# Residual stream of a hybrid layer with tokens on partitions; activations as the stationary operand in both output passes and the output projection; token chunks 272/384/384

## The chip, the cores and the metric

One core of a Trainium2 chip runs the whole layer. The metric is the device time of one launch in microseconds (us), the median of several runs; less is better. The core's engines work side by side and wait for one another by semaphores: TensorE (PE) multiplies matrices and writes to PSUM; VectorE (DVE), ScalarE (ACT) and GpSimd (POOL) work elementwise; SyncE (SP) issues most transfers, one after another, to the DMA engines. In a matmul, PE holds one operand of up to 128 x 128 (the stationary one, loaded by PEld) and streams the other (the moving one) column by column, up to 512 columns, into a PSUM tile.

## The reference

One layer for 1024 tokens of width 1024, with 16 learned tokens ahead of them (1040 rows in all), in float32:

```python
h = h + 0.5 * swiglu(rms_norm(h, ffn1_norm), ffn1_w_in, ffn1_w_out)
u = rms_norm(h, mix_norm) @ w_in
o = concat([hgrn2(...), stick_breaking(...)])     # two groups of heads, 512 columns each
h = h + o @ w_out
h = h + 0.5 * swiglu(rms_norm(h, ffn2_norm), ffn2_w_in, ffn2_w_out)
return h[:, 16 tokens on]
```

`swiglu` is `(silu(g) * u) @ w_out` with `g, u` the halves of `h @ w_in`; the FFN's inner width is 2816. The two mixers' insides are the same before and after.

## The kernel before

Every operand of a large product is split into a high and a low part ("wh, wl" for weights, "xh, xl", "th, tl" for activations: a cast on ACT, a subtraction on DVE), and each product is three matmuls (high x high, high x low, low x high). So each weight tile goes from its raw buffer (an SP transfer) through ACT (L277, L516, L148) and DVE (L279, L518, L150) to PE.

The residual stream is kept with the model's width on partitions: `hT` holds eight tiles of 128 features by all tokens. Tokens are cut into three chunks by `THIRDS` (352, 344 and 344 with the 16 learned ones in the first). The first FFN runs one chunk plainly, and the other two as a pair with seven products in place of eight: the operands are combined blocks (B11, B21, B22, T1 to T4; weights A11, A12, A22, S1 to S4), named after the step. Its stages in order:

- Input products, `fast_in`: for each weight tile the plain chunk (bank `qd`) and the pair (banks `qa`, `qb`, `qc`), 12 matmuls each. Meanwhile `turn_x` (L711) turns x by PE transposes (L721) into `xD` in DRAM.
- Output pass, `fast_out`: first `plain_round` (L554, 22 rows of weights with 24 matmuls each), then the seven products, each over 11 pairs of weight rows `q` (L588). The weights are stationary, the activations move; four PSUM tiles hold 4 x 128 features by 344 tokens, and at a step's end four DVE operations add them to `hT` (L598). `load_h` fetches `hT` from `xD` in eight transfers of 520 KB. Row sums for the norm (`norm_steps`) come from squares on ACT (L210), sums on DVE (L211), a PE product with a column of ones (`nps`, L176) and a PE product that spreads the result over partitions (`spread`, L199); the scaled result is split in two (L1449, L1454). `project_early` then begins the mixers' projections.
- Mixers, with a hand-set weave of PE work. `mix_out` (L1228) multiplies `o` by `w_out`: the first half (four heads, `oT`) is woven into the mixers' work, the second half (`oH`) follows, for each 128 columns `m` and for two token halves of 512. Its result goes to `hT` and `h2D` (DRAM). Weights of the second half come through the pool "wo2" with two raw buffers (`raw`, L141).
- Second FFN, over two token halves of 512 by the seven products alone: `blocks_a` and `blocks_b` make the combined blocks out of normed `hT`, `fast_in` and `fast_out` as above with 512 columns, and `store_out` (L732) turns the result by PE transposes (L739) into rows and stores it, after the steps S3 and A22.

PE's order is the order in which the code issues its work (`manual_schedule`); the other engines get theirs from a scheduler, and pools reuse memory, so that a transfer can wait for the last reader of what lay in its place. SP's queue is served in order: a transfer that waits holds up those behind it.

Of the kernel before, what the change touches and what calls it, by code (L numbers as in the profile page):

```python
# [28 lines left out]
THIRDS = [(0, 352), (352, 344), (696, 344)]  # L29
# [10 lines left out]
class Block:  # L40
# [19 lines left out]
    def setup(self):  # L60
# [19 lines left out]
        self.g2 = self.column(a["ffn2_norm"][0], KT, "g2")  # L80
# [144 lines left out]
    def blocks_a(self, hT, gain, c, n, r, ops):  # L225


        for half, o in enumerate(("B11", "B21")):
            for j in range(4):
                self.halve(ops[o], self.normed(hT, gain, 4 * half + j, c, n, r), j)  # L230
                yield

    def blocks_b(self, hT, gain, cs, n, r, ops, pool):

        nc = self.nc
        sub = nc.vector.tensor_sub
        b11, b21 = ([hT[:, k + j, cs[0] : cs[0] + n] for j in range(4)] for k in (0, 4))
        b12, b22, t2 = [], [], []  # L240
        for j in range(4):
            b12.append(self.normed(hT, gain, j, cs[1], n, r))
            b22.append(self.normed(hT, gain, 4 + j, cs[1], n, r))
            sub(b11[j], b12[j], b11[j])
            t2.append(pool.tile([P, n], F32, tag="nsq", name="t2", bufs=4))
            sub(t2[j], b22[j], b11[j])
            self.halve(ops["T2"], t2[j], j)
            if j < 3:
                yield
        for j in range(4):  # L250
            sub(b21[j], b21[j], t2[j])
        yield
        for j in range(4):
            sub(b12[j], b22[j], b12[j])
            self.halve(ops["T3"], b12[j], j)
        yield
        for o, b in (("T1", b11), ("T4", b21), ("B22", b22)):
            for j in range(4):
                self.halve(ops[o], b[j], j)
            yield  # L260
# [228 lines left out]
    def fast_out(self, hT, cs, n, w_out, actD, load_h, ready, between=lambda a, q: None,  # L489
# [6 lines left out]
        nq = D_FF // 256  # L496
        sk = op.tile([P, nq, 512], F32, name="sk")
# [46 lines left out]
        def plain_round():  # L544
            c0, n0 = plain
# [14 lines left out]
            for m in range(KT):  # L560
                h = hT[:, m, c0 : c0 + n0]
                nc.vector.scalar_tensor_tensor(h, ps[m], 0.5, h, ALU.mult, ALU.add)
# [12 lines left out]
        for bank, a, b, start, (i, j) in steps:  # L575
            if start:
                banks[bank] = [
                    pout.tile([P, n], F32, tag=f"{bank}{m}", name="o") for m in range(4)
                ]
            for q in range(nq):  # L580
                wh, wl = halved(left(a, q), "w", 512)
                xh, xl = halved(right((q, b), n), "t", n)
                order = [(m, e) for m in range(4) for e in range(3)]
                if a == "A12" and q == 0:
                    order.sort(key=lambda me: me[1])
                for m, e in order:
                    y, z = ((wh, xh), (wl, xh), (wh, xl))[e]
                    nc.tensor.matmul(  # L588
                        banks[bank][m], y[:, m * P : (m + 1) * P], z,
# [6 lines left out]
            for m in range(4):  # L596
                h = hT[:, 4 * i + m, cs[j] : cs[j] + n]
                self.evicted = nc.vector.scalar_tensor_tensor(  # L598
                    h, banks[bank][m], 0.5, h, ALU.mult, ALU.add
                )  # L600
            ready(a)
# [109 lines left out]
    def turn_x(self, pool, xD):  # L711

        nc = self.nc
        for r0 in range(0, T, P):
            m = min(P, T - r0)
# [15 lines left out]

    def store_out(self, hT, pool, pps, c0, n, tag):  # L732
        nc = self.nc
        for i, r0 in enumerate(range(c0, c0 + n, P)):
            for q in range(2):
                row = pool.tile([P, 512], F32, tag="orow", name="orow", bufs=4)
                ps = pps.tile([P, 4, P], F32, tag=f"{tag}{(2 * i + q) % 4}", name="o")
                for k in range(4):
                    nc.tensor.transpose(ps[:, k, :], hT[:, 4 * q + k, r0 : r0 + P], self.ident)  # L739
                dst = row.rearrange("p (k c) -> p k c", k=4)  # L740
                if q == 0:
# [593 lines left out]
    def run(self):  # L1335
# [20 lines left out]
        with ExitStack() as c0:  # L1356
            with ExitStack() as c1:
# [54 lines left out]
                with tc.manual_schedule(engines={nc.tensor.engine}), ExitStack() as c2:  # L1412
# [97 lines left out]
                    for _ in range(5):  # L1510
                        next(last)
# [205 lines left out]
```

## Time and profile before

| | |
|---|---|
| median of 3 runs | 2102.15 us (2101.22 to 2105.67) |
| span of the profiled execution, first to last instruction | 2101.1 us |
| lowest run, against that span | 0.1 us more |
| mean granted TensorE clock | 0.994 |
| 0 to 60 us, start: PE busy | 44.59 us |
| 60 to 500, first FFN's input products: PE busy | 436.21 us |
| 745 to 1380, projections and mixers: PE busy | 608.17 us |
| 1380 to 1430, second half of the output projection: PE busy, DVE busy | 46.77, 36.82 us |
| 1475 to 1875, second FFN's input products after their start: PE busy | 395.39 us |
| 1875 to 2066, second FFN's output pass: PE busy, DVE busy | 187.77, 136.55 us |

A line of the profile names an engine, a source line, the operation and its tiles as out<-in. In the chain of work, a row is "start, duration, what": the chain is followed back from the last instruction to what released it, so a row of DVE or DMA there is a time in which PE waited. In rows by stretches of time, each engine's busy time stands with its count of instructions; then the granted clock, the share of the DMA engines and GB/s. "idle <-" or "[... <-]" names what ended the wait before an instruction.

### The profile page before, as it was taken

To read this page: it belongs to the slowest core of one execution; us is meant where nothing else is said; L and a number is where in the kernel's file an instruction comes from. 1 tells how busy PE (TensorE), PEld (TensorE's weight loads), DVE (VectorE), ACT (ScalarE), POOL (GpSimd) and SP (SyncE) were. 2 spreads that over 40 slices of the span, in tenths; PEclk is the share of its full clock that TensorE was granted. 3 is DMA by queue.
4 is the path that set the end of the run, shared out by engine and by line. 5 is a ranking of instruction groups with operands and counts; after the bars stand their busy time and mean duration, and the time that the engine had idled before them with its cause. 6 is when DMAs were issued, how large, how long until landed. Compare 5 with 4: busy or idle time off the path is not lost.

```text
span 2101.1 us, 32170 instructions
## 1 busy us (share of the span) xinstructions
PE 2028.4 (97%) x11520; PEld 1830.6 (87%) x11520; DVE 1392.3 (66%) x2140; ACT 901.4 (43%) x1860; POOL 647.1 (31%) x710
## 2 busy tenths in 40 slices
PE   7999999999999999999999998998999999999998
PEld 6999999999999999988897887886788888878887
DVE  6875544555489942258878776659776676677674
ACT  8543333333465634456666514235233233234443
POOL 2475545452000002243334200012554464430000
PEclk9999999999999999999999999999999999999999
DMA  7643333325867635435454162234533332358364
GB/s 198 190 146 121 110 111 104 98 80 197 254 207 223 220 116 166 156 108 138 119 142 131 51 242 87 81 118 135 162 103 100 111 105 91 107 193 267 111 200 136
DMA packets 272566, 301.12 MB, mean 143 GB/s; under 512 B 24694, under 2 KB 199158, under 8 KB 272406
## 3 DMA queue, kind: packets, MB, share of 16 engines
q1 hardware_dynamic: 254710, 248.62, 39.1%
q0 software_dynamic: 16656, 50.44, 6.5%
q8 instruction: 91, 1.49, 0.3%
q14 instruction: 69, 0.57, 0.1%
q10 hardware_dynamic: 1040, 0.00, 0.0%
HBM read 216.42 MB, written 82.57 MB: 142 GB/s over the span
## 4 chain that ended last, share of the span: by engine, by line
PE 83%; DVE 7%; ACT 2%; issue 1%; DMA 0%; POOL 0%; SPq 0%; DVEq 0%; ACTq 0%; POOLq 0%
PE o L588 16%; PE qb L320 13%; PE qc L320 9%; PE qa L320 8%; PE qd L320 6%; PE proj L163 5%; PE proj L164 5%; PE proj L165 5%; PE o L554 4%; PE flip L1070 2%; PE lvl L839 2%; PE wo L164 1%; PE wo L163 1%; PE wo L165 1%; DVE keep L1216 1%
## 5 line engine op out<-in xcount | busy, mean ns | idle before, releaser
L320 PE MATMUL qb<-T,wh 128*128 128x344 f32 (+1 forms) x1056 | 311.6, 358 | 9.7 <-DVE u L362 5.8
L279 DVE TENSOR_TENSOR wl<-s,wh 128x512 fp32r<-128x512 f32 x176 | 202.5, 1151 | 112.6 <-ACT wh L277 109.9
L588 PE MATMUL o<-tl,wh 128*128 128x344 f32 (+1 forms) x616 | 219.1, 357 | 5.1 <-DVE tl L518 5.1
L320 PEld LDWEIGHTS qb<-T,wh 128*128 128x128 f32 x1056 | 193.0, 189 | 35.3 <-ACT wh L277 7.5
L588 PE MATMUL o<-th,wl 128*128 128x344 f32 (+1 forms) x616 | 218.8, 357 | 2.5 <-DVE wl L518 2.5
L588 PE MATMUL o<-th,wh 128*128 128x344 f32 (+1 forms) x616 | 218.6, 357 | 0.0
L320 PE MATMUL qa<-B,wh 128*128 128x344 f32 (+1 forms) x704 | 209.3, 361 | 0.0
L277 ACT CAST wh<-s 128x512 fp32r<-128x512 f32 x176 | 109.4, 622 | 224.5 <-PE qb L320 154.6
L163 PE MATMUL proj<-xh,wh 128*128 128x344 f32 (+2 forms) x576 | 204.9, 356 | 0.0
L164 PE MATMUL proj<-xh,wl 128*128 128x344 f32 (+2 forms) x576 | 199.5, 346 | 1.1 <-DVE wl L150 1.1
L165 PE MATMUL proj<-xl,wh 128*128 128x344 f32 (+2 forms) x576 | 198.7, 345 | 0.0
L279 DVE TENSOR_TENSOR wl<-raw,wh 128x512 fp32r<-128x512 f32 x172 | 153.4, 896 | 68.1 <-ACT wh L277 61.9
L277 ACT CAST wh<-raw 128x512 fp32r<-128x512 f32 x172 | 105.8, 620 | 194.0 <-PE qc L320 96.0
L320 PE MATMUL qb<-T,wl 128*128 128x344 f32 (+1 forms) x528 | 188.3, 357 | 0.0
L320 PE MATMUL qd<-X,wh 128*128 128x352 f32 x704 | 180.5, 324 | 1.3 <-DVE X L665 1.3
L516 ACT CAST th<-act 128x512 fp32r<-128x512 f32 (+2 forms) x176 | 95.2, 542 | 182.3 <-PE o L588 126.6
L292 POOL TENSOR_TENSOR s<-raw 128x512 f32<-128x512 f32 x88 | 125.0, 1421 | 94.4 <-DVE wl L279 70.1
L518 DVE TENSOR_TENSOR tl<-act,th 128x512 fp32r<-128x512 f32 (+2 forms) x176 | 105.7, 604 | 68.6 <-ACT th L516 68.6
L320 PEld LDWEIGHTS qa<-B,wh 128*128 128x128 f32 x704 | 128.6, 189 | 16.1
L588 PEld LDWEIGHTS o<-tl,wh 128*128 128x128 f32 x616 | 116.6, 190 | 19.3 <-DVE tl L518 6.9
L1216 DVE TENSOR_TENSOR_SCAN keep<-keep 128x144 f32<-128x144 f32 (+6 forms) x112 | 128.5, 1150 | 6.5 <-ACT keep L1212 4.4
L588 PEld LDWEIGHTS o<-th,wl 128*128 128x128 f32 x616 | 116.4, 189 | 15.9 <-DVE wl L518 3.8
(329 smaller groups left out, 4886.7 us busy)
## 6 DMA issues: line engine op xcount, KB each, us to landing
raw<-in_ffn_w_in_dram SPq DMA_DIRECT2D x208, 256.0 KB, 3.1
raw<-in_ffn_w_out_dram SPq DMA_DIRECT2D x176, 256.0 KB, 3.9
raw<-in_w_in_dram SPq DMA_DIRECT2D x28, 512.0 KB, 4.3
ks<-kD SPq DMA_DIRECT2D x32, 260.0 KB, 5.2
ak<-in_ffn_w_out_dram SPq DMA_DIRECT2D x22, 256.0 KB, 4.2
v<-vD SPq DMA_DIRECT2D x8, 576.0 KB, 5.0
hT<-xD SPq DMA_DIRECT2D x8, 520.0 KB, 7.5
xD<-xts POOLq DMA_DIRECT2D x16, 256.0 KB, 2.9
```

The lines of the kernel that those rows point to most:

```text
L163: nc.tensor.matmul(ps, wh[:, s], xs, start=k == 0, stop=False)
L164: nc.tensor.matmul(ps, wl[:, s], xs, start=False, stop=False)
L165: nc.tensor.matmul(ps, wh[:, s], xl[:, k, c0 : c0 + n], start=False, stop=k == nk - 1)
L277: nc.scalar.copy(hi, src)
L279: nc.vector.tensor_sub(lo, src, hi.bitcast(F32))
L292: op(t, x, y)
L320: nc.tensor.matmul(ps, a[:, k, :], b[:, k0 + k, :], start=start and k == 0 and i == 0, stop=k == 3 and i == 2, skip_group_check=True,)
L516: nc.scalar.copy(hi, src)
L518: nc.vector.tensor_sub(lo, src, hi.bitcast(F32))
L554: nc.tensor.matmul(ps[m], y[:, s], z, start=f == 0 and e == 0, stop=f == D_FF // P - 1 and e == 2,)
L588: nc.tensor.matmul(banks[bank][m], y[:, m * P : (m + 1) * P], z, start=start and q == 0 and e == 0, stop=q == nq - 1 and e == 2, skip_grou ...
L1216: nc.vector.tensor_tensor_scan(out=kv, data0=kv, data1=kv, initial=1.0 if last else keep[:, end : end + 1], op0=ALU.mult, op1=ALU.bypass,)
```

## The change

From the first FFN's seven products on, the residual stream is kept with tokens on partitions: `hN`, blocks of 128 tokens by 1024. Six such blocks are loaded straight from x; only the plain chunk, now 272 tokens, still goes through `turn_x` and `hT`, and its two blocks of tokens are turned at the end of its norm (L1449). The pair's chunks have 384 tokens, three blocks each.

In the seven products of both output passes the operands change roles: 128 tokens of the activation are stationary, 512 columns of weights move. The output projection does the same. The norm of a block becomes a row norm (`row_norm`: one ACT square with a row sum, a root, a reciprocal, one DVE operation over 1024 columns with a gain row that is fetched for all partitions), after which PE turns the block by eight transposes (`row_turn`, L247). In the second half of the output projection the order is by block of tokens, and within it by half of the columns. `blocks` makes the second FFN's combined blocks out of the turned and normed `whole`. The result is stored straight from its rows; `store_out` is gone.

```diff
-THIRDS = [(0, 352), (352, 344), (696, 344)]
+THIRDS = [(0, 272), (272, 384), (656, 384)]
...
-                order = [(m, e) for m in range(4) for e in range(3)]
+                order = [(m, e) for m in range(nb) for e in range(3)]
...
-                        banks[bank][m], y[:, m * P : (m + 1) * P], z,
+                        banks[bank][m], z[:, m * P : (m + 1) * P], y,
...
-            for m in range(4):
-                h = hT[:, 4 * i + m, cs[j] : cs[j] + n]
+            for m in range(nb):
+                h = out_of(i, j, m)
...
+    def row_norm(self, h, gain, pool, out=None):
...
+        nc.scalar.activation(junk, h, AF.Square, accum_out=s)
+        nc.scalar.activation(s, s, AF.Sqrt, bias=self.eps, scale=1.0 / D)
+        nc.vector.reciprocal(s, s)
...
+        nc.vector.scalar_tensor_tensor(t, h, s, gain, ALU.mult, ALU.mult)
...
+    def row_turn(self, t, pool, tag, bufs, q):
...
+            self.nc.tensor.transpose(ps[:, k, :], t[:, c : c + P], self.ident)
...
                     def load_h():
                         for k in range(KT):
                             nc.sync.dma_start(hT[:, k, :], xD[k])
+                        for b in range(6):
+                            r0 = n0 - META + b * P
+                            nc.sync.dma_start(hN[:, b, :], a["x"][0][r0 : r0 + P])
...
-        for m, half in plan:
+        for i, b in plan:
...
+                    pn = self.pool("norm2", ctx=c1)
+                    gain = self.gain_row(a["ffn2_norm"][0:1], pn, "g2r")
                     self.weights("wo2", 2, KT, c1)
...
+                    plan = [(i, b) for b in range(KT) for i in range(2)]
+                    turns = [normed(b) for b in range(KT)]
...
-    def store_out(self, hT, pool, pps, c0, n, tag):
...
+                        nc.sync.dma_start(
+                            self.out[0, r0 : r0 + P, 512 * i : 512 * i + 512], out_of(i, j, m)
+                        )
```

What moves in the queues is seen at three places.

**SP at the plain round.** Rows of SP's queue, line, tile<-source, size and count ("raw" weights, "act" activations); before:

```order
L506 DMA raw<-in_ffn_w_out_dram 128x512 x2
L511 DMA act<-act1p_103 128x352
L511 DMA act<-act1p_104 128x352
L511 DMA act<-act1p_105 128x352
L1428 DMA hT<-xD 128x1040 x8
L506 DMA raw<-in_ffn_w_out_dram 128x512 x6
```

and after the change:

```order
L500 DMA raw<-in_ffn_w_out_dram 128x512 x2
L505 DMA act<-act1p_102 128x272
L505 DMA act<-act1p_103 128x272
L505 DMA act<-act1p_104 128x272
L1418 DMA hT<-xD 128x272 x8
L1421 DMA hN_5498<-in_x_dram 128x1024 x6
L500 DMA raw<-in_ffn_w_out_dram 128x512 x9
```

The one burst has become two kinds of transfers, at the same place between the same weights.

**SP at the second half of the output projection.** Before (`res` is the residual of the first half; the last row belongs to the second FFN):

```order
L1248 DMA res<-hD 128x512 x4
L141 DMA raw<-in_w_out_dram 128x4x128 x8
L284 DMA raw<-in_ffn_w_in_dram 128x4x128 x17
L1690 DMA hT_14120<-h2D 128x512 x8
L284 DMA raw<-in_ffn_w_in_dram 128x4x128
```

and after, with `g2r` the gain row:

```order
L1602 DMA oT<-oD 128x4x128
L1237 DMA res<-h1N 128x512
L142 DMA raw<-in_w_out_dram 128x512
L226 DMA g2r<-in_ffn_norm_dram 128x1024
L142 DMA raw<-in_w_out_dram 128x512 x7
L277 DMA raw<-in_ffn_w_in_dram 128x4x128 x96
```

The gain row stands between the first weight tile and the seven others, and no residual is fetched among the second FFN's weights.

**DVE at the start of the second input products.** After the change its rows, from the combined block T1 (`T_15646` with its high part `T_15645`; `T_15648` is T4, `B_15650` B22, `t_...` are the steps towards T2) to the first weights that are a difference (`s`):

```order
L272 TENSOR_TENSOR wl<-raw,wh 128x512
L222 TENSOR_TENSOR T_15646<-whole,T_15645 128x512 x4
L1696 TENSOR_TENSOR whole<-whole,t_15752 128x512
L1696 TENSOR_TENSOR whole<-whole,t_15757 128x512
L1696 TENSOR_TENSOR whole<-whole,t_15762 128x512
L417 TENSOR_TENSOR sg<-qa,sg 128x512
L222 TENSOR_TENSOR T_15648<-whole,T_15647 128x512 x3
L1696 TENSOR_TENSOR whole<-whole,t_15767 128x512
L222 TENSOR_TENSOR B_15650<-whole,B_15649 128x512 x2
L222 TENSOR_TENSOR T_15648<-whole,T_15647 128x512
L222 TENSOR_TENSOR B_15650<-whole,B_15649 128x512 x2
L272 TENSOR_TENSOR wl<-s,wh 128x512 x3
```

All combined blocks stand ahead of the first difference weights; those over T2 and T3 are further up.

More of the change, by code (lines that the diff above doesn't have):

```diff
@@ L1 @@
 from contextlib import ExitStack
-from itertools import chain, islice
+from itertools import chain, islice, repeat
 import numpy as np
@@ L577, in fast_out @@
                 banks[bank] = [
-                    pout.tile([P, n], F32, tag=f"{bank}{m}", name="o") for m in range(4)
+                    pout.tile([P, 512], F32, tag=f"{bank}{m}", name="o") for m in range(nb)
                 ]
@@ L730, in turn_x @@
                 yield
-    def store_out(self, hT, pool, pps, c0, n, tag):
[L733 to L741, printed above, removed]
-                    nc.scalar.copy(dst, ps)
-                else:
-                    nc.vector.tensor_copy(dst, ps)
-                nc.sync.dma_start(self.out[0, r0 : r0 + P, 512 * q : 512 * q + 512], row)
     def project(self, xh, xl, col, chunks, use, w=None):
```

358 lines of the change are left out of this document (198 added, 160 removed).

## The prediction

> **What bounds the kernel now.** I read the page first (shares, then the chain of work that ended last), then the longest pieces of that chain, then busy time by stretches of time, and last the chain in detail at four places.
>
> ```profile
> span 2101.1 us, 32170 instructions
> PE 2028.4 (97%) x11520; PEld 1830.6 (87%) x11520; DVE 1392.3 (66%) x2140; ACT 901.4 (43%) x1860; POOL 647.1 (31%) x710
> PE 83%; DVE 7%; ACT 2%; issue 1%; DMA 0%; POOL 0%; SPq 0%; DVEq 0%; ACTq 0%; POOLq 0%
> ```
>
> TensorE (PE) is busy 97% and makes 83% of the chain, VectorE (DVE) 7%. So nearly every matmul counts at its pace, and what else counts are the few places where PE waits. The pace is read from long unbroken pieces of the chain (start, duration, line, count):
>
> ```profile
> 163.63 1.92 PE qd L320 x12
> 502.70 83.90 PE o L554 x525
> 615.89 98.61 PE o L588 x631
> 1879.74 175.31 PE o L588 x765
> 2061.93 29.96 PE o L588 x132
> ```
>
> One matmul takes 160 ns at 352 columns (83.90/525; 1.92/12 says the same), 156.3 ns at 344 (98.61/631), 227.0 ns at 512 (29.96/132). From 344 to 512 that is 0.421 ns a column. My estimate for the new widths on this line: 384 columns 173.1 ns, 272 columns 126.0 ns. The second lies below the measured pieces, but one pair of matmuls of that width is in the trace:
>
> ```profile
> 951.38 0.28 PE L1206 MATMUL z<-ks,qs 128*128 128x272 f32 x1
> 951.50 0.28 PE L1207 MATMUL z<-ks,qs 128*128 128x272 f32 x1
> 951.63 0.23 PE L1209 MATMUL z<-neg_b,ident_b 128*128 128x128 bf16 x1
> 147.61 0.44 PE xt L721 x4
> ```
>
> They start 0.12 and 0.13 us apart, so 126 ns is reachable with a new stationary operand each time. The last row prices a 128-column transpose: 0.11 us.
>
> **Sum, part by part** (after minus before, on PE's path).
>
> *First input products.* 1056 matmuls of the plain chunk go from 160 to 126.0 ns: -35.9 us; 1848 of the seven products from 156.3 to 173.1: +31.0. Together **-4.9**. 12 matmuls of 126 ns last 1.5 us and still cover one weight split of 0.6 us on DVE, so I add no wait.
>
> *Turning x.* 72 transposes at L721 become 24 (8 of them small): 48 x 0.11 = **-5.3**.
>
> *Plain round of the output pass.* 528 x (126.0 - 159.8) = -17.8. What covers it now is the DMA, and that cover gets thin:
>
> ```profile
> 500.24 3.91 SPq L1428 DMA_DIRECT2D hT<-xD  x8
> 505.84 13.71 SPq L506 DMA_DIRECT2D raw<-in_ffn_w_out_dram  x6
> 517.85 0.62 ACT L516 CAST wh<-raw 128x512 fp32r<-128x512 f32 x1 [3.45 <-PE o L554]
> 500.00:588.00 88.00, 87.87 (x552) 87.58 (x551) 44.80 (x75) 37.62 (x72) 9.87 (x16) 1.00 0.81 265
> ```
>
> A burst of 4.2 MB (hT) goes out at 500.24 with nine weight tiles ahead of it; the tenth is issued at 505.84 and split from 517.85 on, 15.2 us after PE's piece began at 502.70. Its matmuls come after 108 others, 17.3 us at 159.8 ns: just in time. The new burst (hT of 272 tokens plus six x blocks) has the same bytes and the same place in the queue, while PE gets there in 13.6 us; with the split that is a wait of about 3.6 us. Over the whole round the last row says 0.81 of the DMA engines for 88 us, 71 us of transfers; a round of 67 us has little room. I take +4 (bounds 0 and +7): **-13.8**.
>
> *Seven-product output pass.* 924 matmuls of 344 columns become 693 of 512: 693 x 227.0 - 924 x 156.3 = +12.9. Block turns add 48 transposes and the first chunk's blocks 16: +7.1. Norm sums and spreads of two chunks go (12 + 12 matmuls between 0.13 and 0.20 us by the rows at 1430.60 and 1432.63 below): -2.5 with a little left over elsewhere. PE idles now 4.2 us in this stretch:
>
> ```profile
> 588.00:745.00 157.00, 152.76 (x963) 150.42 (x962) 146.06 (x292) 91.89 (x192) 9.26 (x18) 0.99 0.67 208
> ```
>
> DVE works 146 of 157 us here, so its wide norm steps between the splits are what PE waits for. They turn into one 1024-wide step per block; I take 3 us of this and neighbouring waits off. Sum **+14.5** (bounds +11 to +19, as none or twice that goes).
>
> *Second half of the output projection (oproj).* Here I see the largest new wait. The weights come through two raw buffers, and a pair of splits costs a fixed turn-round:
>
> ```profile
> L141 SPq DMA_DIRECT2D raw<-in_w_out_dram x8: 367/368/426, 1373.7 to 1392.7; - x8
> 1376.97 2.89 DMA raw<-in_w_out_dram
> 1381.49 1.41 DVE wl L150
> 1382.95 0.50 PE wo L164
> 1385.74 0.62 ACT L148 CAST wh<-raw 128x512 fp32r<-128x512 f32 x1 [4.29 <-DMA raw<-in_w_out_dram]
> 1386.57 0.62 ACT L148 CAST wh<-raw 128x512 fp32r<-128x512 f32 x1 [0.21 <-DMA raw<-in_w_out_dram]
> 1390.45 0.62 ACT L148 CAST wh<-raw 128x512 fp32r<-128x512 f32 x1 [0.60 <-DMA raw<-in_w_out_dram]
> 1394.72 0.63 ACT L148 CAST wh<-raw 128x512 fp32r<-128x512 f32 x1 [0.80 <-DMA raw<-in_w_out_dram]
> PE wo L164 <- DVE wl L150: 1.5, 1, 1.5
> ```
>
> ACT's casts of the pairs start at 1385.74, 1390.45 and 1394.72: 4.3 to 4.7 us per pair (2.89 transfer, 0.62 cast, about 0.69 subtraction, which frees the buffer). Today a split feeds 12 matmuls in a row (2.7 us), more than half a pair's time, and the loads began at 1373.7, before the first half's last matmuls; PE waited 1.5 us. After the change the first block of tokens needs all eight splits within its 24 matmuls, three to each. And seven of the eight loads stand on SP behind the gain row g2r, which is put where the first half's residual tiles lie, so it can go only about 1 us after the first half's last matmul, T. Counting on by hand from these durations: first split T+3.7 (transfer, cast, subtraction), second 7.3, third 8.0, then one pair per 4.3 us, the eighth T+20.4. Block 0 ends at T+20.9 where its matmuls alone need 5.4: +15.4, less the 1.5 waited now, **+13.9**. Bounds: +3 if the loads were as early as now, +16 at 4.7 us a pair. Behind it, seven blocks of 5.4 us cover DVE's and ACT's work per block.
>
> *What the clock adds.* Where PE has waited for about 3 us, the matmuls after it run slow:
>
> ```profile
> 1464.63 5.47 PE qb L320 x12
> 1465.00:1475.00 10.00, 9.75 (x31) 7.30 (x31) 9.63 (x15) 2.49 (x4) 1.51 (x1) 0.71 0.69 210
> ```
>
> Twelve matmuls take 5.47 us in place of 2.72 after a wait from 1461 on, with a granted clock of 0.71. I add +2 for the first matmuls after the long wait of block 0 (0 to +5). The Trainium skill, "TensorE: Matmul & The Clock Gate", section "Why this matters for your kernels", says that gaps over about 3 us between bursts of matmuls bring the clock back to half for a window. The trace agrees at 1464.63; read strictly, the rule would spare block 0, whose waits between pairs are 2.9 us by my count, and its sum would be 2 us lower.
>
> *Norm of the second FFN.* 56 block transposes before the second half ends (6.2 us), less the first chunk's norm sum and spread (2.65 by the rows below): **+3.5**.
>
> *Start of the second input products.* From the end of the projection (1428.38) the rows are:
>
> ```profile
> 1430.60 1.07 PE nps L176 x8
> 1432.63 1.58 PE spread L199 x8
> 1434.21 10.90 PE qa L320 x42
> 1448.02 1.70 DVE wl L279
> 1449.72 1.71 DVE t L246
> 1453.28 0.60 DVE wl L279
> 1461.61 1.68 DVE T L223
> ```
>
> PE's first product over a combined block starts at 1464.63, 36.2 us after the projection, and DVE is what it waits for: steps of 0.60 us each, some of them 1.7. After the change the first weights are no longer loaded ahead, as their buffers lie under the oproj weights, and DVE makes all combined blocks, 42 steps of 0.60 us, before the first subtraction for difference weights. By hand: block 7's eviction, norm and turn take until some T2+10 (T2 the end of the projection), the 42 steps 25 us, four weight subtractions among them 2.4: the subtraction comes at about T2+38, the product over T3, the one that starts at 1464.63 now, 3 us later, and 3 us later still if three steps are stretched as in these rows: T2+44. So +7.6, of which I take 2.5 back, as the next combined blocks are then already there: **+5** (0 to +12).
>
> *Second output pass.* Matmuls the same; 4 MB of residual now stand behind six pairs of loads at its start, and PE has 16 us of work ahead of the seventh: 0 (0 to +3).
>
> *Output.* The 64 transposes and their copies go:
>
> ```profile
> 2056.43 2.40 DVE hT L598 x4
> 2058.87 3.05 PE o L739 x25
> 2091.89 0.77 PE o L739 x7
> 2094.68 2.49 DMA out_dram<-orow
> ```
>
> Between steps 5.5 us (2056.43 to 2061.93) shrink to about 1 for the evictions that free the banks. At the end, 9.2 us after the last product (2091.89 to 2101.1) shrink to some 5: four evictions of 0.6 and one transfer of 2.5. **-8.5**.
>
> Sum: -4.9 - 5.3 - 13.8 + 14.5 + 13.9 + 2 + 3.5 + 5 - 8.5 = **+6.4 us**. On the profiled execution's 2101.1 that is 2107.5; the median of the runs shown, 2102.15, lies 1.05 above that span, so I say **2108.5**.
>
> **Rivals.** (1) *The oproj weights come earlier.* If the second half's loads get out some 7 us before T, as now (1373.7 against casts from 1380.3), and not behind g2r, the first pair is split before T and the eighth split is there at about T+10 (three more pairs of 4.3 us): block 0 waits 5 us and not 15, and the clock stays up: 2108.5 - 12 = **2096.5**, faster. For it: today's loads do start early. Against it: the first raw tile lies on a weight tile of the first half and g2r on its residual tiles. (2) *DVE decides the start of the second FFN.* If the stretched steps (1.7 for 0.60) fall on nine of the 42 and not on three, the product over T3 is another 6 to 7 us late: **2115**. It decides once the chain from T2 exceeds what PE has to do meanwhile, 96 matmuls and the first weights' wait, some 30 us. For it: three of the four DVE rows above are stretched; against: GpSimd, whose additions run beside them, has no more to do than now. (3) *Narrow matmuls don't reach 126 ns*, since each brings a new stationary operand: PEld's 87% busy speaks for it, the pair at 951.38 and the transposes at 0.11 against. At 145 ns, (1056 + 528) x 19 ns = +30: **2138**. (4) *The change's waits are hidden by half*, the ones of the oproj and of the second FFN's start: 2108.5 - 7 = **2101.5**, no difference.
>
> **How the numbers follow.** The forecast has 0.40, with its own range 2103 to 2114; rival 1 has 0.24, rival 2 0.17, rival 3 0.03, rival 4 0.16. A measurement of this kernel tells about 0.2% (4.2 us) from no change: 2098 to 2106.4. Faster: rival 1, 0.24. Same: rival 4 and the lower third of the forecast, 0.16 + 0.14 = 0.30. Slower: the rest, 0.46. The range leaves out rival 3 and the outer tails of 1 and 2: 2093 to 2119.
>
> **What would show it.** Right: in the chain, a plain round of about 70 us with one wait of 3 to 4 us at its fifth row of weights; a stretch of some 15 us after the last matmul of the oproj's first half in which PE is a quarter busy and waits for DVE's subtractions behind pairs of 4.3 us; a wait of 5 to 10 us before the first difference product of the second FFN; nothing but four evictions and a transfer after the last matmul. Wrong: oproj weights already split when the second half begins (then about 2096), a cadence at 272 columns above 130 ns, or PE waits inside the seven products longer than the 4.2 us of now.

## The result and the profile after

Before: 2102.51 us, median of 4 runs (2101.22 to 2105.67). After: **2118.11 us**, median of 4 runs (2117.8 to 2121.03). The ratio is 1.0071, with a 95% interval of 1.0056 to 1.0085: 15.6 us slower. The forecast was 2108.5, so its side was right, its range (2093 to 2119) held the time, with 0.9 us to spare, and its size was 9 us too small.

The profiled execution of after is the slowest of its four (2121.03), 2.9 us above the median, so the stages below add up to 18.1 us and not to 15.6. Its page begins with the span and the busy time of each engine (microseconds, share of the span, instructions), and its part 4 has the shares of the chain that ended last:

```profile
span 2119.2 us, 31494 instructions
PE 2028.9 (96%) x11249; PEld 1795.3 (85%) x11249; DVE 1373.6 (65%) x2067; ACT 902.8 (43%) x1854; POOL 624.8 (29%) x676
PE 80%; DVE 6%; DMA 2%; ACT 2%; issue 2%; POOL 0%; DVEq 0%; SPq 0%; ACTq 0%; POOLq 0%
```

PE has as much busy time as before (2028.9 against 2028.4 us) with 271 matmuls fewer; yet its share of the chain falls from 83% to 80%, and DMA, which had no whole per cent, now has 2%. So the 18.1 us by which the spans differ are mostly time in which PE waits or is held up. By stages (us; predicted terms put in the stage they fall into). T is the start of the last product of oproj's first half (1380.45 before, 1380.29 after), T2 the end of the projection (1428.4, 1447.6); the other bounds are the starts of PE's first matmul of a stage:

| stage | before | after | difference | predicted |
|---|---|---|---|---|
| up to the plain round of the first output pass | 501.93 | 497.99 | -3.9 | -10.2 |
| plain round | 84.5 | 67.0 | -17.5 | -13.8 |
| seven products, up to T | 794.0 | 815.3 | +21.3 | +14.5 |
| T to T2, oproj's second half with its norm and turns | 47.9 | 67.3 | +19.4 | +19.4 |
| T2 to the second output pass | 443.6 | 451.7 | +8.1 | +5 |
| second output pass and output | 229.2 | 219.9 | -9.3 | -8.5 |

The term of oproj's second half is right, the last stage nearly. The others miss by +6.3, -3.7, +6.8 and +3.1. Single executions differ by a little: in the seven traces of kernels whose first stage is that of after, it ends between 496.7 and 499.0.

Two long pieces of the chain of after (start, duration, line, count) give the new paces; the third row is the end of the chain:

```profile
498.69 66.45 PE o L548 x525
623.11 53.16 PE o L582 x233
2113.31 2.73 DVE hN L592 x4
```

66.45/525 is 126.6 ns at 272 columns, 53.16/233 is 228 ns at 512: both as priced from one pair of matmuls and one long piece of before. The plain round is one unbroken piece, and behind the last product stand only four evictions and, up to 2119.2, a transfer, as predicted.

**Block 0 of oproj's second half.** ACT's timeline shows the casts of the weight tiles (start, duration, line, what; in brackets the idle time before it and what ended it):

```profile
1383.11 0.62 ACT L147 CAST wh<-raw 128x512 fp32r<-128x512 f32 x1 [2.85 <-DMA raw<-in_w_out_dram]
1386.87 0.62 ACT L147 CAST wh<-raw 128x512 fp32r<-128x512 f32 x1 [3.14 <-DMA raw<-in_w_out_dram]
1387.65 0.62 ACT L147 CAST wh<-raw 128x512 fp32r<-128x512 f32 x1 [0.17 <-DMA raw<-in_w_out_dram]
...
1399.13 0.62 ACT L147 CAST wh<-raw 128x512 fp32r<-128x512 f32 x1 [0.74 <-DMA raw<-in_w_out_dram]
```

With the first half's last matmul at about T = 1380.3 and 1.3 us for cast and subtraction, the first split is ready at T+4.1, the next two at T+7.9 and T+8.7, the eighth at T+20.1. The hand count said T+3.7, 7.3, 8.0 and 20.4. SP's timeline gives the reason that was named too (the gain row, then seven loads), and the windows show PE in it (bounds, length, busy time and count of PE, PEld, DVE, ACT and POOL, granted clock, DMA share, GB/s):

```profile
1380.05 0.34 SPq L142 DMA_DIRECT2D raw<-in_w_out_dram  x1
1381.44 0.33 SPq L226 DMA_DIRECT2D g2r<-in_ffn_norm_dram  x1
1381.82 14.73 SPq L142 DMA_DIRECT2D raw<-in_w_out_dram  x7
```

```profile
1380.00:1400.00 20.00, 11.74 (x24) 5.86 (x24) 6.36 (x10) 5.20 (x9) 2.17 (x2) 0.65 0.42 132
1400.00:1410.00 10.00, 10.00 (x42) 7.88 (x42) 4.33 (x7) 3.70 (x8) 0.70 (x2) 0.85 0.13 54
```

24 matmuls in 20 us, which alone are 5.4 us of work at 227 ns. Their 11.74 us of busy time are stretched by a clock of 0.65 (0.50 from 1388 to 1400). While they wait for splits anyway this should cost little by itself; that is argued, not tested.

**The start of the second input products.** The chain there, in order of time:

```profile
1477.36 0.61 DVE wl L272
...
1478.01 7.19 PE qa L313 x23
...
1485.90 1.88 DVE T L222 x3
1487.79 0.60 DVE whole L1696
1488.39 1.20 DVE B L222 x2
1489.59 0.60 DVE T L222
1490.20 1.20 DVE B L222 x2
1491.40 0.61 DVE wl L272
...
1492.06 4.24 PE qb L313 x11
...
1497.15 2.99 PE qb L313 x12
```

PE stands twice. Up to 1478.01 it waits for the low part of a raw weight tile, which DVE makes behind the blocks of T2 and part of those of T3; up to 1492.06 for the low part of the first difference weights, which DVE makes behind every combined block. Both rows at `qb` up to 1497 belong to the product over T2 (its first matmul ran at 1485.02); the one over T3 starts at 1497.15. The list of waits (engine, line, awaited; total, times, longest) names two of them:

```profile
PE qb L313 <- DVE wl L272: 6.6, 1, 6.6
PE qa L313 <- DVE wl L272: 5.0, 1, 5.0
```

DVE's block steps also begin late. The chain before them:

```profile
1447.64 2.92 DMA raw<-in_ffn_w_in_dram
...
1451.25 8.96 PE qa L313 x24
...
1461.34 0.75 DVE whole L1684 x2
```

The first weights are loaded only at the end of the projection, and the turn of the last block of tokens stands on PE (at 1460.04) behind 24 products with these weights. Those take 8.96 us where 24 at 227 ns take 5.4, with a granted clock of 0.57 between 1450 and 1458. So the first block step comes 13.7 us after T2.

**The seven products.** PE idles more, not less. First the windows of the whole piece, then of 25 us in it (columns as above), and the waits in those 25 us:

```profile
565.00:737.00 172.00, 165.50 (x747) 134.98 (x746) 142.60 (x260) 93.70 (x187) 3.90 (x8) 1.00 0.62 197
600.00:625.00 25.00, 21.87 (x102) 17.21 (x101) 16.82 (x29) 11.26 (x22) 2.18 (x4) 1.00 0.83 258
```

```profile
PE o L582 <- DVE wl L512: 1.9, 2, 1.3
PE hb L1449 <- ACT hbs L1453: 1.2, 1, 1.2
```

6.5 us idle in 172 against 4.2 in 157 before. (In six other kernels below with the same products and turns it is 4.0 to 6.6 us, so a part of the 6.5 belongs to this execution.) Half of it, 3.1, lies between 600 and 625, where the turns of the first chunk's rows (hb) and their stores were put. The chain shows the weights' transfers there at 4 to 5 us each, around the time of those stores (602 to 612):

```profile
601.23 5.27 DMA raw<-in_ffn_w_out_dram
...
608.09 4.31 DMA raw<-in_ffn_w_out_dram
...
613.21 4.87 DMA raw<-in_ffn_w_out_dram
```

**The plain round's missing wait.** SP's timeline shows when the burst of hT and x blocks is issued:

```profile
488.89 3.77 SPq L1418 DMA_DIRECT2D hT<-xD  x8
493.09 3.97 SPq L1421 DMA_DIRECT2D hN<-in_x_dram  x6
502.37 12.10 SPq L500 DMA_DIRECT2D raw<-in_ffn_w_out_dram  x9
```

It goes out 9.1 us ahead of the round (497.99), where it went 1.7 us ahead before (500.24 against 501.93). The bytes have 7 us more to land before the round begins, and the round ran without a wait. What the burst itself waited for on SP, before and then after:

```profile
SPq L1428 <- DVE wl L279: 4.5, 1, 4.5
SPq L1428 <- PE qc L320: 4.0, 1, 4.0
```

```profile
SPq L1418 <- PE qb L313: 1.0, 1, 1.0
```

### The profile page after: what moved, and what is told of

Read it like the earlier page. It is cut to its first block, busy times and chain, and to the rows that moved or that the text cites. A ratio compares the mean times of both kernels' runs of the same rounds, so it can differ in the third digit from the quotient of the medians.

```text
span 2119.2 us, 31494 instructions
## 1 busy us (share of the span) xinstructions
PE 2028.9 (96%) x11249; PEld 1795.3 (85%) x11249; DVE 1373.6 (65%) x2067; ACT 902.8 (43%) x1854; POOL 624.8 (29%) x676
## 4 chain that ended last, share of the span: by engine, by line
PE 80%; DVE 6%; DMA 2%; ACT 2%; issue 2%; POOL 0%; DVEq 0%; SPq 0%; ACTq 0%; POOLq 0%
PE o L582 15%; PE qb L313 14%; PE qc L313 9%; PE qa L313 9%; PE proj L162 5%; PE proj L164 5%; PE proj L163 5%; PE qd L313 4%; PE wo L1232 4%; PE o L548 3%; PE flip L1051 2%; PE lvl L820 2%; DMA raw<-in_ffn_w_out_dram 1%; DVE keep L1197 1%; PE oacc L1121 1%
## 5 line engine op out<-in xcount | busy, mean ns | idle before, releaser
L313 PE MATMUL qb<-T,wh 128*128 128x384 f32 (+1 forms) x1056 | 320.4, 364 | 5.8 <-DVE u L355 5.8
L313 PE MATMUL qa<-B,wh 128*128 128x384 f32 (+1 forms) x704 | 217.4, 371 | 3.6 <-ACT wh L270 3.6
L582 PE MATMUL o<-wl,th 128*128 128x512 f32 x539 | 210.4, 392 | 4.2 <-DVE wl L512 4.2
L582 PE MATMUL o<-wh,tl 128*128 128x512 f32 x539 | 210.0, 391 | 3.5 <-DVE tl L512 3.5
L582 PE MATMUL o<-wh,th 128*128 128x512 f32 x539 | 210.5, 392 | 0.0
L272 DVE TENSOR_TENSOR wl<-raw,wh 128x512 fp32r<-128x512 f32 x178 | 165.0, 930 | 63.7 <-ACT wh L270 60.3
L162 PE MATMUL proj<-xh,wh 128*128 128x384 f32 (+2 forms) x576 | 205.4, 357 | 0.2 <-ACT xh L252 0.2
L163 PE MATMUL proj<-xh,wl 128*128 128x384 f32 (+2 forms) x576 | 199.6, 346 | 0.0
L164 PE MATMUL proj<-xl,wh 128*128 128x384 f32 (+2 forms) x576 | 199.2, 346 | 0.1
L313 PE MATMUL qb<-T,wl 128*128 128x384 f32 (+1 forms) x528 | 192.7, 365 | 6.6 <-DVE wl L272 6.6
L313 PE MATMUL qd<-X,wh 128*128 128x272 f32 x704 | 146.1, 294 | 1.3 <-DVE X L661 0.9
```

Of the source, the lines that this page charges most:

```text
L162: nc.tensor.matmul(ps, wh[:, s], xs, start=k == 0, stop=False)
L163: nc.tensor.matmul(ps, wl[:, s], xs, start=False, stop=False)
L164: nc.tensor.matmul(ps, wh[:, s], xl[:, k, c0 : c0 + n], start=False, stop=k == nk - 1)
L272: nc.vector.tensor_sub(lo, src, hi.bitcast(F32))
L313: nc.tensor.matmul(ps, a[:, k, :], b[:, k0 + k, :], start=start and k == 0 and i == 0, stop=k == 3 and i == 2, skip_group_check=True,)
L582: nc.tensor.matmul(banks[bank][m], z[:, m * P : (m + 1) * P], y, start=start and q == 0 and e == 0, stop=q == nq - 1 and e == 2, skip_grou ...
```

## The experiments

Each ratio is to the kernel before in the same rounds, each gain is the difference of medians to the 2118.11 of the kernel after. Executions of one kernel lie up to 7 us apart, and the median of the kernel before moved between 2102.51 and 2104.00 from round to round, so a gain of some 2 us is not clear by itself. Where the stage that an edit touches says more in the traces, its length stands beside the gain.

**Block 0: more raw buffers, the gain row behind the weights.**

```diff
-                    gain = self.gain_row(a["ffn2_norm"][0:1], pn, "g2r")
-                    self.weights("wo2", 2, KT, c1)
+                    late = {}
+                    self.weights("wo2", 4, KT, c1)
...
-                        t = self.row_norm(hN[:, b, :], gain, pn, px)
+                        if not late:
+                            late["g"] = self.gain_row(a["ffn2_norm"][0:1], pn, "g2r")
+                        t = self.row_norm(hN[:, b, :], late["g"], pn, px)
```

> Edit: four raw buffers in place of two for the weights of the oproj's second half, and the gain row g2r fetched behind them in SP's queue. Theory A (two buffers and the gain row set block 0's wait): by the chain of 4.3 us a pair, block 0 ends at about T+10.7 in place of T+20, PE's waits there fall from some 13 us to 3 to 5, and the kernel takes 8 to 11 us less than the changed kernel (2107 to 2110 us). Rival B (the loads wait for the memory of the first half's last tiles, or ACT and DVE set the pace): the waits keep 10 us or more, and the gain is under 3 us.

Measured: 2107.79 us, 1.0029 [1.0018, 1.0040]: 10.3 us gained. T to T2 takes 58.0 us in place of 67.3. In SP's queue the gain row now stands behind four of the eight loads. Its waits at block 0 and the window of 20 us from its own T (columns as above):

```profile
PE wo L1232 <- ACT wh L147: 4.0, 2, 3.3
PE wo L1232 <- DVE wl L149: 0.2, 1, 0.2
```

```profile
1377.63:1397.63 20.00, 15.76 (x62) 11.60 (x61) 10.08 (x16) 8.22 (x15) 2.46 (x3) 0.91 0.47 159
```

62 matmuls fit in the 20 us that held 24. So most of what the weights' order and buffers cost is shown. The two halves of the edit apart:

> Edit: four raw buffers for the weights of the oproj's second half; the gain row stays where the change put it, behind the first of the eight loads. Theory A1 (the two-buffer turn-round is most of block 0's wait): gain 7 to 8 of the 10 us of both edits together, 2110 to 2111 us; the second split still comes some 3.6 us after the first. Rival (the gain row's place in the queue is most of it): gain under 4 us.

> Edit: the gain row g2r behind the eight weight loads, two raw buffers as in the change. Theory A1 (turn-round): the pairs come 3 us earlier at most, gain 1 to 3 us (2115 to 2117). Rival (gain row's place): gain 6 us or more.

Four buffers alone: 2113.59, 1.0044 [1.0031, 1.0056], 4.5 us gained, less than the 7 to 8 expected. The gain row late alone: 2117.09, 1.0059 [1.0046, 1.0071], 1.0 us, which is within the noise. The stage itself is steadier than the whole time. T to T2 takes 67.3 us in after and 66.7 to 67.5 in four other traces with the same loads; 67.1 with the gain row late, 60.3 with four buffers, 58.0 with both, and 57.8 to 60.2 in the five later kernels with both. So the two buffers are most of it, 7 us, as expected; the gain row's place shows nothing alone, and some 2 us on top of four buffers, which one of the six traces with both doesn't have. SP's timelines of the two, four buffers first:

```profile
1380.08 0.33 SPq L226 DMA_DIRECT2D g2r<-in_ffn_norm_dram  x1
1380.46 7.92 SPq L142 DMA_DIRECT2D raw<-in_w_out_dram  x7
```

```profile
1382.37 10.68 SPq L142 DMA_DIRECT2D raw<-in_w_out_dram  x6
```

With four buffers seven loads still stand behind g2r until 1380.46. In the other run g2r goes behind the first two loads, and the six others still wait for one of two buffers, until 1382.37: the buffers hide the little that the gain row's place is worth.

**Second FFN: combined blocks as they are needed.** The residual's tile gets a pool that stays, and the blocks are handed out one by one between the products.

```diff
-                    whole = px.tile([P, KT, SEQ], F32, name="whole")
+                    whole = pw.tile([P, KT, SEQ], F32, name="whole")
...
+                        sub(b21[j], b21[j], t2[j])
...
+                    yield
...
-                        sub(b21[j], b21[j], t2[j])
...
-                    ops, n, a["ffn2_w_in"][0], actD, 2, ev0, open_ev, repeat(None)
+                    ops, n, a["ffn2_w_in"][0], actD, 2, ev0, open_ev, made
...
-                next(made)
...
-                next(made)
...
-                drain(made)
```

> Edit: the second FFN's combined blocks T2, T3, T1, T4 and B22 are made one after another as the products ask for them, not all ahead of the first products over T2 and T3; the work is the same. Theory A (DVE's order decides: difference weights stand behind 42 steps): PE's two waits of 5.2 and 6.8 us at the start of the second input products fall to 4 us or less together, the clock drop behind them with them, gain 7 to 10 us (2108 to 2111). Rival B (DVE's amount of work decides): the same wait comes in two or three smaller ones before the later products, gain under 3 us.

Measured: 2110.12, 1.0033 [1.0020, 1.0045]: 8.0 us gained. T2 to the second output pass takes 441.9 us in place of 451.7. The waits of 6.6 and 5.0 for the weights' low parts are replaced by:

```profile
PE qb L313 <- DVE u L355: 4.4, 1, 4.4
```

So the blocks made too early were the cost, and DVE's evictions of the first products are next in line.

**Seven products: the first chunk's rows turned in a later round.** The same turns and stores, advanced in the step S2 and not in S1.

```diff
+                    def first_rows():
...
+                            norms["rows"] = first_rows()
...
+                        elif step == "S2":
+                            if q % 2:
+                                next(norms["rows"], None)
```

> Edit: the four turns of the first chunk's blocks (hb) and their 1 MB of stores move from the step S1 to the step S2 of the first FFN's output pass. Theory A (the stores take S1's transfers the room): the waits behind weight transfers at 606 to 623 us go, gain 3 to 4 us (2114 to 2115). Rival B (S1's own two weight tiles and one activation per 2.0 us, 0.73 MB, are what the DMA can't carry): the waits stay within 1 us, gain under 1 us.

Measured: 2116.01, 1.0061 [1.0047, 1.0074]: 2.1 us gained where 3 to 4 were expected, not clear as a time. The stage is clearer: the seven products take 167.1 to 168.5 us in the six traces with this edit and 169.4 to 173.9 in the seven without it, with 2.5 to 3.3 us of idle time in place of 4.0 to 6.6. The window that corresponds to 600 to 625:

```profile
599.00:624.00 25.00, 25.00 (x112) 20.69 (x111) 21.85 (x39) 12.47 (x25) 0.00 (x0) 1.00 0.82 253
```

PE has no gap left in it. The DMA share is the same as before the edit (0.82 against 0.83): this load on the DMA engines by itself doesn't make PE wait; the turns and stores in this round did. Which of the two weighs more was not separated.

**The start: fewer openers.** The plain chunk's first products ("openers") run while DVE and ACT make the first combined blocks. The change itself raised them from three pairs to four (and the loop below from 3 to 5), which the prediction's sum doesn't price; this edit takes that back.

```diff
-                        ops, nw, a["ffn1_w_in"][0], act1D, 4, ev0, open_ev, None, plain, between
+                        ops, nw, a["ffn1_w_in"][0], act1D, 3, ev0, open_ev, None, plain, between
...
-                    for _ in range(5):
+                    for _ in range(3):
```

> Edit: three opening pairs of the plain chunk in place of four at the start, as before the change. Theory A (the fourth opener loads DVE with eight more weight splits while the first blocks are made): PE's waits in the first 200 us fall from 17 to about 11 us, gain 4 to 6 us (2112 to 2114). Rival B (matmuls of 272 columns leave DVE too little time per split, whatever the openers): the waits stay or grow, since PE comes to the combined blocks 12 us earlier; no gain, or up to 5 us slower.

Measured: 2119.34, 1.0074 [1.0061, 1.0087], no difference that shows (1.2 us more). PE's waits in the first 80 us grew from 17.5 to 20.1 us, where a fall from 17 to about 11 was expected; that theory fell.

**The start: longer openers.** Two extra matmuls in each of 32 opener products, which count low parts twice; 8.1 us of PE work, none for another engine.

```diff
+                if k == 3:
+                    for j in range(extra):
+                        nc.tensor.matmul(
+                            ps, wl[:, j, :], xh[:, k0 + j, :], start=False, stop=False,
+                            skip_group_check=True,
+                        )
...
-                    ps = alone(ps, operand(block(i, h, col)), h, h == 0)
+                    ps = alone(ps, operand(block(i, h, col)), h, h == 0, 2)
```

> Edit: the changed kernel, with two matmuls of 272 columns more (low part of the weights by the first two blocks of x, a second time) in each of the 32 products of the four opening pairs: 64 x 0.126 = 8.1 us more for PE at the start, nothing for the other engines; this part of the result counts the low parts twice. Theory A (the start goes at the pace of DVE and ACT, so shorter matmuls there don't count): PE's waits between 25 and 75 us shrink and the time grows by 4 us or less against the changed kernel's 2118.1. Rival B (PE's matmuls set the start, and the missing 6 us of the first stage lie elsewhere): 7 to 8 us more, 2125 to 2126.

Measured: 2126.10, 1.0108 [1.0091, 1.0125]: 8.0 us lost. The first stage itself ends 5.9 us later (503.9 against 498.0), so by the stage three quarters of PE's own work count there, by the time all of it. The largest wait, for the low parts of the weights, between 25 and 75 us; of after, then of this kernel:

```profile
PE qd L313 <- DVE wl L272: 4.1, 4, 2.9
```

```profile
PE qd L319 <- DVE wl L272: 2.6, 2, 2.4
```

It shrinks by 1.5 us, and all of PE's waits in this stretch from 7.7 to 5.4, for 8.1 us of cover: for the most part PE doesn't wait there for a steady supplier.

**All three gains together.**

> Edit: four raw buffers, gain row late, combined blocks as needed, first chunk's rows in S2, all together. If the waits are separate, the gains add up: 10 + 8 + 2 = 20 us off the changed kernel, 2097 to 2099 us, which is 4 to 6 us under the kernel before. If one wait takes another's place (the second FFN's first weights, whose buffers lie under the oproj's), 2102 or more.

Measured: **2097.88, 0.9973 [0.9962, 0.9984]**. 20.2 us gained; the single gains sum to 10.3 + 8.0 + 2.1 = 20.4. This version is faster than both kernels, by 0.3% (5.7 us) than the one before in the same rounds. The next four runs start from it.

**With it, five openers** (the same two numbers as above, 5 and `range(7)`):

> Edit: as the last, with five opening pairs of the plain chunk in place of four. With three openers the start's waits grew by 5 us and the time by 1. If DVE's fixed work on the first blocks is what PE waits for, a fifth opener gives PE 96 more matmuls (12 us) to do meanwhile: its waits in the first 100 us fall from 12 to some 6 us and the time by 1 to 4 us against the kernel without it. If each opener brings DVE as much work as it gives PE, no difference within 1 us.

Measured: 2099.75, 0.9980 [0.9971, 0.9989]: no gain. The waits at the start are the same; each opener brings DVE a subtraction too.

**With it, low parts of every second opener made by GpSimd.**

```diff
-            nc.vector.tensor_sub(lo, src, hi.bitcast(F32))
+            eng.tensor_sub(lo, src, hi.bitcast(F32))
...
-                    ps = alone(ps, operand(block(i, h, col)), h, h == 0)
+                    ps = alone(ps, operand(block(i, h, col), (nc.vector, nc.gpsimd)[h]), h, h == 0)
```

> Edit: as the kernel with all three mends (four raw buffers and gain row late, blocks as needed, rows in S2), and every second weight tile of the four opening pairs has its low part subtracted on GpSimd in place of DVE: 16 of DVE's steps of 0.6 us go. Theory A (DVE bounds the start): PE's waits in the first 75 us, 17 us there, fall by 3 us or more, and the time by 2 to 4 us (2094 to 2096). Rival B (ACT, 24 of 25 us busy between 25 and 50, bounds it, or GpSimd's steps hold DVE up): within 1 us, or slower.

Measured: 2111.40, 1.0044 [1.0031, 1.0058], 13.5 us worse than without, where a gain of 2 to 4 was expected. The group of these subtractions (busy us, mean ns, idle before) and the wait they cause, both up to 490 us:

```profile
L272 POOL TENSOR_TENSOR wl<-raw,wh 128x512 fp32r<-128x512 f32 x16 | 22.9, 1435 | 29.7 <-ACT wh L270 28.0 <-issue 1.7
```

```profile
PE qd L313 <- POOL wl L272: 7.9, 4, 4.6
```

One takes 1.44 us against 0.60 to 0.68 on DVE. PE waits 7.9 us for them. Of the 13 us by which the first stage grew, another 4.7 are 47 more matmuls of the plain chunk that took about 227 ns in place of 126; the granted clock is 0.86 from 50 to 100 us, where it is 0.93 and then 1.00 without the edit.

**With it, five splits ahead**, and the control that gives up the same raw buffers alone:

```diff
-            hi = wp.tile([P, 4, P], F32R, tag="wh", name="wh", bufs=3)
+            hi = wp.tile([P, 4, P], F32R, tag="wh", name="wh", bufs=5 if plain else 3)
...
-            lo = wp.tile([P, 4, P], F32R, tag="wl", name="wl", bufs=3)
+            lo = wp.tile([P, 4, P], F32R, tag="wl", name="wl", bufs=5 if plain else 3)
...
-                    self.t_bufs, self.in_bufs = 2, 8
+                    self.t_bufs, self.in_bufs = 2, 5
```

> Edit: as the kernel with all three mends, with five buffers for the split weights of the first FFN's input products in place of three (and five raw weight buffers in place of eight, to make room). Theory A (DVE can be only three splits ahead, 4.6 us of matmuls at 272 columns against 5.8 at 352, and is held up longer than that by the first blocks): PE's waits for DVE's subtractions between 25 and 75 us fall from 4.3 us to under 1.5, the first stage ends 3 to 5 us sooner than without the extra buffers. Rival B (the splits wait for ACT's casts or the first blocks themselves): the first stage within 1 us.

> Edit: the control of the last: all three mends, five raw weight buffers in place of eight in the first FFN's input products, three split buffers as before. Both theories: no more than 2 us slower than with eight, as four tiles are in use at a time and one is loaded ahead; what is lost here has to be added to what the five split buffers show.

Measured: five splits 2112.66, 1.0039 [1.0026, 1.0053]; the control 2102.38, 0.9993 [0.9985, 1.0002]. So the lost raw buffers cost 4.5 us, more than the 2 expected, and the deeper splits another 10.3, of which 7.0 are in the first stage (511.1 against 504.0). Waits between 25 and 75 us with five splits:

```profile
PE xps L629 <- DVE row L651: 7.5, 3, 4.0
PE qd L313 <- DVE wl L272: 1.4, 1, 1.4
```

The subtractions were indeed waited for less (1.4 against 3.8 without the edit and 4.4 in the control). But PE waited 7.5 us for the first block's rows, which DVE makes too; 4.1 of these 7.5 are in the control as well, so they come with the lost raw buffers. The extra splits taking DVE's time from the rows would explain the other 3.4; that is argued.

## Why the prediction was right or wrong

The total is right in its sign and its range, and part of that is luck: the misses of the stages, +6.3, -3.7, +6.8, 0, +3.1 and -0.8, cancel in part, and the time lies above the 2103 to 2114 of the forecast's own path.

*First input products, -4.9, and turning x, -5.3: mis-sized by 6.3.* The paces were right: the seven products of this stage took 30.3 us more (31.0 predicted), the transposes 4.3 less (5.3 predicted). The step that failed is "so I add no wait": the plain chunk's products came down by 30.4 us, not 35.9. Each counted up to PE's next start, they take 142.1 us, 1056 x 126 ns being 133.1; so 9.0 us are no pace, against 3.5 before (172.5 less 1056 x 160 ns). They are not all waits. Some 4.5 us are gaps (1.8 before), and 3.5 are 35 matmuls that took about 227 ns in place of 126 without a gap (8 slow ones and 0.8 before). All of it lies in the first 85 us; in the 672 later matmuls of the plain chunk the comparison of 12 matmuls with one subtraction of 0.6 us holds. At the start DVE and ACT also make rows, norms and combined blocks (DVE is busy for 24.2 of the 25 us from 50 on, but was so before), which the comparison leaves out. The runs show what doesn't help: more or fewer openers, GpSimd, deeper splits. Why gaps and slow matmuls grew by 5 to 6 us and not by more or less stays open.

*Plain round, -13.8: the +4 of wait didn't come.* The step "the new burst has ... the same place in the queue" was right by its place, but the burst is issued 11.4 us earlier. In the code its destination no longer lies where the last weight split of the input products is read. SP's waits agree: 4.5 us for that split's subtraction (L279) and 4.0 for a product of the pair before, 1.0 for a product of the pair after. No run tested it by itself. The pace alone gives 528 x (126.6 - 159.8) = -17.5, which is what was measured.

*Seven products up to oproj, +14.5: mis-sized by 6.8.* The pace was as counted. The step that failed is "I take 3 us of this and neighbouring waits off": PE's idle time in the products rose from 4.2 to 6.5, which makes 5.3 of the 6.8. It is also what the prediction named as a sign that it is wrong. The wide norm steps on DVE did go, and the turns of the first chunk's rows with their stores came in their place; moving them recovered 2.1 us of the time, about 4 of the stage. The norm's 24 matmuls, at the prices of the rows that the prediction names, are 4.0 us and not 2.5, so the sum should have been 1.5 lower. What is left, some 3 us, lies behind the last of the seven products, where the way to T takes 643.0 us against 639.0 before (640.6 to 643.4 in the other traces); it was not tracked down.

*Oproj, +13.9, and clock, +2: right in mechanism and time.* Every step of the hand count is within 0.7 us of the trace. The experiments show the two raw buffers as the reason; the gain row in front of the loads, the other one named, is worth at most some 2 us. PE's rate behind block 0 bears out the clock's term: the 42 matmuls from 1400 to 1410 include eight turns of 0.11 us, so at full pace they are some 8.5 us of work in 10, and the clock's visible price is about 1.5 there. On the rule of the Trainium skill, "TensorE: Matmul & The Clock Gate", section "Why this matters for your kernels", block 0 can't decide: its longest single wait was 3.1 us, right on the gap of about 3 us that it names. But in the kernel before the granted clock fell to 0.71 (738 to 742) after two waits of 1.8 and 1.7 us, so here shorter waits did it too, and the measurement decides.

*Norm, +3.5: right.* With the two terms above it makes the 19.4 us from T to T2.

*Start of the second FFN, +5: mis-sized by 3.1, and closer than its steps.* Three DVE steps were stretched, as counted (1.69 to 1.71 for 0.60 before 1475). But "until some T2+10" was 13.7, because the last block's turn stands behind 24 slow products on PE; the first difference weights' subtraction came at T2+43.8, not 38 to 41, and the product over T3 49.5 us after T2, not 44. That is 13.3 us later than before, where 7.6 was predicted. Of this 5.2 came back up to the second output pass (2.5 predicted), which leaves the 8.1.

*Output, -8.5:* -9.3, right.

*Rivals.* The oproj weights did not come earlier (1): with the loads made faster by hand, block 0 gave 9 to 10 us back, not far from the 12 that this rival priced. DVE took three stretched steps, not nine (2). The narrow matmuls do reach 126 ns (3). The waits were not hidden (4). The forecast's own path held in its mechanisms; what it lacked were waits and slow matmuls in stages that it priced by pace alone, and the late start of the second FFN's blocks.

## What to carry to other kernels

When a matmul gets shorter, recount every supplier of the stage in its own time: one split against twelve matmuls held where the engine had only splits to make, and not at the start, where it had other work due. A change of layout moves memory as well, and with it the moment when a load may start: here it cost some 9 us at one place (late loads through two buffers) and took away, at another, a wait priced at 4. Read a small edit by the stage that it touches: two buffers more gained 7 us of their stage and 4.5 of a time that scatters by several. Waits in separate stages add up (20.4 singly, 20.2 together).

## What the runs showed of the hardware

A DVE step with two operands in SBUF, 0.60 us in the chain above, takes 1.7 us beside a GpSimd operation (1470 to 1475 in after) and can take more. DVE's timeline and then GpSimd's in the kernel before:

```profile
1876.26 3.43 DVE L518 TENSOR_TENSOR tl<-act,th 128x512 fp32r<-128x512 f32 x1
```

```profile
1876.65 1.27 POOL L443 TENSOR_TENSOR t<-sg,t 128x512 f32<-128x512 f32 x1
1877.87 1.26 POOL L450 TENSOR_TENSOR sg<-sg 128x512 f32<-128x512 f32 x1
```

3.43 us is the duration of 0.68 plus 2.75, about two GpSimd operations (2.53). The Trainium skill, "SBUF — State Buffer", section "SBUF: two separate sides", says that such a DVE step and a GpSimd operation that reads SBUF lock each other out for a whole instruction. The wait in these rows agrees with it: the DVE step ends 0.56 us after the second GpSimd operation. Who started first doesn't show in them, as by the profile it is the DVE step (1876.26 against 1876.65). The lost 13.5 us of the run with GpSimd's subtractions may have it as a part, which was not tested.

In block 0 the granted clock was 0.50 from 1388 to 1400 although PE stood for no more than 3.1 us at a time: waits of 3.1 and 2.3 us came first, then three of 0.7 to 1.0 us with four to six matmuls between them. The full pace was back at 1403.2, after PE had worked without a wait from 1398.4 on. In the kernel before, two waits of 1.8 and 1.7 us (up to 732 and 736) were followed by 0.71 from 738 to 742.
